# A transformer block whose merge of the memory branch is stored by accumulation, with VectorE's order written out at two stage borders

## The chip, the cores and the metric

The kernel runs on one core of a Trainium2 chip. The metric is the device time of one execution in microseconds (us), the median of several runs. One execution was also recorded by the hardware profiler; its page and its trace are what is quoted here. Engines are named as the page names them: PE is TensorE (matmuls; PEld is its weight load), DVE is VectorE, ACT is ScalarE, POOL is GpSimd, SP is SyncE, which only issues DMAs.

## The reference

One layer of a hybrid block, 512 positions of width 2048, all in float32 (cut to what matters here):

```python
h = rms_norm(x, norm_g)
proj = h @ w_in                       # 13 parts, among them the gates g_conv, g_mla, g_mem
...
o_conv = (b_gate * causal_conv(c_gate * u) * silu(conv_z)) @ w_conv_out
o_mla  = (mla_attention(...) * silu(mla_z)) @ w_mla_out
o_mem  = (memory_attention(...) * silu(mem_z)) @ w_mem_out
merged = sigmoid(g_conv) * o_conv + sigmoid(g_mla) * o_mla + sigmoid(g_mem) * o_mem
x = x + merged @ w_o
```

## The kernel before

**Products.** Every float32 operand is split into two parts that TensorE takes: whi (rounded, by ScalarE) and wlo (the rest, by VectorE, which subtracts whi). A product is three matmuls (L161 whi·xhi, L162 whi·xlo, L163 wlo·xhi). The large products (input projections from w_h, mla_out, w_o) go by panels with seven instead of eight products per 2×2 block: VectorE first forms sums of the raw weight blocks (L263 to L265), then ScalarE rounds (L268) and VectorE subtracts (L269). The left operand goes through the same (pair_sums L243 to L246, pair_split L249 and L250). A panel has four chunks of 42 matmuls, and its results are taken out of four banks (L304 to L314) once all chunks are done. The smaller products (memory K/V, conv_out, mem_out) have plain weights (L154, L155).

**Weights in flight.** SP loads raw weights into three buffers; whi and wlo have two each. `queue` holds the jobs in order, each a generator of two steps (load and sums, then split). `take()` is called at the start of a chunk: it lets the jobs of the next chunks begin, splits the next one, and hands out the weights of the present one. So when chunk k runs, chunk k+1 is split and the sums of k+2 are formed.

**Stages in time.** Memory K/V to about 107 us; input panels (58 of them) to 1320, whose gates go to DRAM (gdram); attention in head groups to 1620 (mla), where the words of ORDER_Q and its like say in which order streams are advanced: `w` a weight product of the next group's projection, `A` and `B` the finishing of old heads, `a` and `b` scores and preparation of new ones; conv_out and memory attention to 1740; mla_out panels to 1908; mem_out in five groups (512, 512, 512, 256 and 256 columns) to 1998; w_o panels to the end. What the three branches add up to lies in DRAM (mgdram): conv_out's results times their gates are stored there (L1040, L1041), mla_out's are added by an accumulating store (L1217, L1218).

**Merge of mem_out.** For each pair of row blocks, `mem_pair` (L1231) loads the gate and the sum so far into one tile "mg" (one buffer), multiplies the banks of mem_out by the gate (L1236), adds the sum so far (L1237), and makes the pair for w_o out of it (sums, then split into xo, L250). It runs step by step beside the next group's matmuls and beside w_o's first panels; xo0 to xo7 are w_o's left operands.

**Who sets the order.** SP and TensorE run in the order in which the program is written (written order, `manual_schedule`); for VectorE a scheduler of the framework sets the order, but for one region of six steps at the first border of the input panels, where the order is the program's. Each engine then works its list in order: an instruction that waits holds up everything behind it. `middle()` of a panel issues the loads of what its results are combined with (gates, the residual xr).

Of the kernel before, what the change touches and what calls it, by code (L numbers as in the profile page):

```python
# [30 lines left out]
P = 128  # L31
# [76 lines left out]
def body(ctx, tc, a, out):  # L108
# [165 lines left out]
    def panel_steps(xp, e, tag, middle=None, tail=None):  # L274
# [235 lines left out]
    def staged_parts():  # L510
# [4 lines left out]
                         (None, None, staged_parts), lambda c: memory_load(c + 1)))  # L515
    work = panels(xp, a["w_h"], len(SEQUENCE), lambda n: make(n), lambda n, e: finish(n, e), "aux")
    queue.insert(32 + 15, [lambda: rotary_weights(), None])
    parts_of_x = all_parts()
    for grp in range(4):
        banks = [bank("acc") for _ in range(2)]  # L520

        for n in dense_units(banks, 512, mT, "T", nk=KB, before=memory_chunk if grp == 0 else None,
                             ahead=lambda c: 2 if 0 < 8 * grp + c - 7 < 23 else 1):
# [39 lines left out]
    for _ in parts_of_x:  # L563
        pass
    close_st()
# [76 lines left out]
    def rotary():  # L642
# [76 lines left out]
        def turned(tag):  # L719
# [4 lines left out]
            nc.gpsimd.dma_start(krdram, kr)  # L724
        later.append(turned)
        yield
# [67 lines left out]
    with tc.manual_schedule(engines={DVE}):  # L794
        for step in range(6):
            next(work)
            if step == 0:
                for i in (6, 7):
                    xp.append(pair_tile(pxb, f"xp{i}"))
                    x_load(i, etile())  # L800
                late_parts = [x_pair(6), x_pair(7)]
            elif step < 5:
                for _ in range(1 + step % 2):
                    next(late_parts[(step - 1) // 2])
# [210 lines left out]

    def gate_blocks(grp):
# [12 lines left out]
        return out  # L1029
# [8 lines left out]
    def conv_result(grp, banks):  # L1038
        for i, sg in enumerate(gate_blocks(grp)):
# [23 lines left out]
    def conv_steps():  # L1063
        for grp in range(4):
            for r in conv_out(grp):
                if r is not None:
                    results[grp] = r
                    if pg is not None:
# [312 lines left out]
```

## Time and profile before

| what | us |
| --- | --- |
| three runs, median (lowest to highest) | 2189.48 (2189.06 to 2191.71) |
| the profiled execution, its time | 2187.3 |
| the profiled execution, its span on the chip | 2185.5 |
| mean granted clock of TensorE in it | 0.992 |

The page begins with each engine's busy time and instruction count. A row of the timeline has start, length, engine, line, operation and out<-in, and in brackets the idle time of the engine just before it and what ended that. A row of the waits has who waited, for whom, the total, the number of times and the longest. A row of the DMA issues has out<-in, queue, count, size and the median time from issue to landing. Here is how the three longest stages with stalls look in the slices of the page, where a digit is the busy share of one fortieth of the span in tenths:

```profile
PE   9989999999999999999999999999999999998799
PEclk9999999999999999999999999999999999999899
```

The dips are in the third slice and in the two slices near the end (mem_out to w_o).

### The profile page before, as it was taken

To read this page: it belongs to the slowest core of one execution; us is meant where nothing else is said; L and a number is where in the kernel's file an instruction comes from. 1 tells how busy PE (TensorE), PEld (TensorE's weight loads), DVE (VectorE), ACT (ScalarE), POOL (GpSimd) and SP (SyncE) were. 2 spreads that over 40 slices of the span, in tenths; PEclk is the share of its full clock that TensorE was granted. 3 is DMA by queue.
4 is the path that set the end of the run, shared out by engine and by line. 5 is a ranking of instruction groups with operands and counts; after the bars stand their busy time and mean duration, and the time that the engine had idled before them with its cause. 6 is when DMAs were issued, how large, how long until landed. Compare 5 with 4: busy or idle time off the path is not lost.

```text
span 2185.5 us, 38852 instructions
## 1 busy us (share of the span) xinstructions
PE 2128.3 (97%) x16040; PEld 2038.7 (93%) x16040; DVE 1741.5 (80%) x2764; ACT 1003.8 (46%) x1219; POOL 123.9 (6%) x173
## 2 busy tenths in 40 slices
PE   9989999999999999999999999999999999998799
PEld 8789999999999999999999999888888799987799
DVE  6986888888888888888888786888877688757787
ACT  6743444344334334444444444877764433323333
POOL 0000000000000000000000001221211100000000
PEclk9999999999999999999999999999999999999899
DMA  8633433333334334343444446222266765554343
GB/s 331 231 106 136 155 136 126 126 126 129 123 126 137 115 129 137 118 141 127 136 136 139 133 136 244 74 82 108 98 231 249 306 186 173 170 204 149 126 147 136
DMA packets 92289, 334.31 MB, mean 153 GB/s; under 512 B 10768, under 2 KB 11024, under 8 KB 90064
## 3 DMA queue, kind: packets, MB, share of 16 engines
q1 hardware_dynamic: 72000, 256.77, 34.4%
q0 software_dynamic: 11616, 51.12, 6.6%
q10 hardware_dynamic: 8496, 23.94, 3.1%
q8 instruction: 125, 2.05, 0.4%
q14 instruction: 52, 0.43, 0.1%
HBM read 273.34 MB, written 58.46 MB: 152 GB/s over the span
## 4 chain that ended last, share of the span: by engine, by line
PE 81%; DVE 8%; DMA 4%; issue 4%; ACT 2%; POOL 0%; SPq 0%; DVEq 0%; POOLq 0%; ACTq 0%
PE acc L161 14%; PE acc L162 14%; PE acc L163 14%; PE aux L163 11%; PE aux L162 11%; PE aux L161 11%; DVE wlo L269 3%; DMA raw<-in_w_mla_out 1%; DMA raw<-in_w_o 1%; DVE raw L263 1%; PE aux L978 1%; DMA sb<-gdram 1%; DMA raw<-in_w_h 1%; PE aux L961 1%; DVE wlo L155 0%
## 5 line engine op out<-in xcount | busy, mean ns | idle before, releaser
L268 ACT ACTIVATE whi<-raw 128x1792 fp32r<-128x1792 f32 x304 | 517.7, 1703 | 793.0 <-PE acc L162 352.8
L269 DVE TENSOR_TENSOR wlo<-raw,whi 128x1792 fp32r<-128x1792 f32 x304 | 614.3, 2021 | 194.2 <-ACT whi L268 193.7
L163 PE MATMUL aux<-xp,wlo 128*128 128x256 f32 (+1 forms) x1712 | 479.5, 280 | 5.0 <-DVE wlo L269 5.0
L161 PE MATMUL aux<-xp,whi 128*128 128x256 f32 (+1 forms) x1712 | 479.8, 280 | 1.0 <-ACT whi L268 1.0
L162 PE MATMUL aux<-xp,whi 128*128 128x256 f32 (+1 forms) x1712 | 480.0, 280 | 0.0
L163 PE MATMUL acc<-xp,wlo 128*128 128x256 f32 x1680 | 469.4, 279 | 3.4 <-DVE wlo L269 3.4
L162 PE MATMUL acc<-xp,whi 128*128 128x256 f32 x1680 | 469.8, 280 | 0.0
L161 PE MATMUL acc<-xp,whi 128*128 128x256 f32 x1680 | 469.3, 279 | 0.0
L163 PEld LDWEIGHTS aux<-xp,wlo 128*128 128x128 f32 (+1 forms) x1712 | 320.4, 187 | 5.6 <-DVE wlo L269 5.6
L161 PEld LDWEIGHTS aux<-xp,whi 128*128 128x128 f32 (+1 forms) x1712 | 321.4, 188 | 1.4 <-ACT whi L268 1.4
L162 PEld LDWEIGHTS aux<-xp,whi 128*128 128x128 f32 (+1 forms) x1712 | 320.9, 187 | 0.0
L163 PEld LDWEIGHTS acc<-xp,wlo 128*128 128x128 f32 x1680 | 314.6, 187 | 4.3 <-DVE wlo L269 4.2
L161 PEld LDWEIGHTS acc<-xp,whi 128*128 128x128 f32 x1680 | 315.6, 188 | 0.0
L162 PEld LDWEIGHTS acc<-xp,whi 128*128 128x128 f32 x1680 | 315.1, 188 | 0.0
L263 DVE TENSOR_TENSOR raw<-raw 128x512 f32<-128x512 f32 x304 | 208.0, 684 | 57.3 <-DMA raw<-in_w_h 29.8
L155 DVE TENSOR_TENSOR wlo<-raw,whi 128x1024 fp32r<-128x1024 f32 (+2 forms) x91 | 101.5, 1119 | 47.7 <-ACT whi L154 47.7
L154 ACT ACTIVATE whi<-raw 128x1024 fp32r<-128x1024 f32 (+2 forms) x91 | 88.9, 977 | 102.6 <-PE acc L162 41.5
L265 DVE TENSOR_TENSOR raw<-raw 128x256 f32<-128x256 f32 x304 | 127.7, 421 | 6.2
L264 DVE TENSOR_TENSOR raw<-raw 128x256 f32<-128x256 f32 x304 | 127.6, 420 | 5.7
L343 POOL TENSOR_TENSOR rs_r<-rs_t,mhalf 128x2 f32<-128x2 f32 (+2 forms) x71 | 69.5, 989 | 270.0 <-DVE rs_t L342 209.6
L161 PE MATMUL acc<-whi,blk 128*128 128x384 f32 (+1 forms) x224 | 84.8, 379 | 0.0
L163 PE MATMUL acc<-whi,blk 128*128 128x384 f32 (+1 forms) x224 | 80.9, 361 | 0.0
(359 smaller groups left out, 3900.9 us busy)
## 6 DMA issues: line engine op xcount, KB each, us to landing
raw<-in_w_h SPq DMA_DIRECT2D x240, 512.0 KB, 3.5
raw<-in_w_mla_out SPq DMA_DIRECT2D x32, 512.0 KB, 3.9
raw<-in_w_o SPq DMA_DIRECT2D x32, 512.0 KB, 3.7
raw<-in_w_mem_kv SPq DMA_DIRECT2D x31, 512.0 KB, 7.2
gdram<-e ACTq DMA_DIRECT2D x22, 512.0 KB, 2.8
raw<-in_w_ukv SPq DMA_DIRECT2D x16, 512.0 KB, 5.6
raw<-in_w_conv_out SPq DMA_DIRECT2D x16, 512.0 KB, 9.0
aadram<-z POOLq DMA_DIRECT2D x8, 896.0 KB, 4.1
```

Source lines behind the costliest of these rows:

```text
L154: act.activation(hi[:, cols], raw[:, cols], AF.Copy)
L155: vec.tensor_tensor(out=lo[:, cols], in0=raw[:, cols], in1=r32(hi[:, cols]), op=ALU.subtract)
L161: nc.tensor.matmul(o, lhsT=s[0], rhs=m[0], start=start, stop=False, skip_group_check=shared)
L162: nc.tensor.matmul(o, lhsT=s[0], rhs=m[1], start=False, stop=False, skip_group_check=shared)
L163: nc.tensor.matmul(o, lhsT=s[1], rhs=m[0], start=False, stop=stop, skip_group_check=shared)
L263: vec.tensor_tensor(out=f[:, 4:6], in0=f[:, 1:3], in1=f[:, 0:1].to_broadcast([P, 2, 256]), op=ALU.add)
L264: vec.tensor_tensor(out=f[:, 6], in0=f[:, 5], in1=f[:, 1], op=ALU.add)
L265: vec.tensor_tensor(out=f[:, 7], in0=f[:, 6], in1=f[:, 3], op=ALU.add)
L268: act.activation(hi, f[:, 1:8], AF.Copy)
L269: vec.tensor_tensor(out=lo, in0=f[:, 1:8], in1=r32(hi), op=ALU.subtract)
L343: pool.tensor_tensor(out=r, in0=t, in1=mhalf[:, :n], op=ALU.pow)
L961: nc.tensor.matmul(sb[:, :n], lhsT=qr[:, cols], rhs=krh[:, :n], start=False, stop=False)
```

## The change

It has eight parts.

1. `take()` gets a list `fills`: pieces of VectorE's work that are put between the split of chunk k+1 and the sums of chunk k+2, one per chunk. The beginning of a job is a function of its own, `begin`.
2. From step 27 of memory K/V to the sixth step of the input panels, VectorE's order is the program's (`manual_dve`). The last two pairs of x (xp6, xp7) are four fills there. Weight buffers of their own ("staged") are used at entries 0, 3, 6 and so on instead of 2, 5, 8, the look-ahead of two starts at step 8 and ends after step 30, and the first panel's jobs begin before the stage's end (`begin(2)`).
3. ORDER_Q, ORDER_Q1 and ORDER_LAST: a weight product stands between `B` and the first score `a`, and in the first group two more products stand ahead of the scores; the later runs of `w` are shorter by as much.
4. A panel's `middle()` is called at its second chunk before the weights are taken, not at the third chunk after.
5. The rotary transposes of the latents are made available one step later (`yield` ahead of `later.append`).
6. The gate loads of conv_out are written apart from the multiplications (`gate_blocks(grp)` fills `gates_of`).
7. The tile "my" of the memory attention has four buffers instead of two.
8. mem_out: each group is multiplied by its gates as soon as it is done (L1277), out of the banks into the gate tile, which is added to mgdram by an accumulating store (L1278). The gates are loaded ahead (L1260) into three slots that take the place of xo7; the sum is read back (L1271) into the places of xo6 and xo5 (pairs 0 to 4), into "merge" (5 and 6) or a tile of its own (7). The pairs are made three steps later. L1237 is gone. VectorE's order is the program's from the beginning of mem_out to the ninth chunk of w_o (n == 8). A w_o panel's addition of the residual becomes a fill.

The diff, without some of the smaller moves:

```diff
-ORDER_Q = "a a a B a a a 4w a w b b 5w a 4w a w a a w"
+ORDER_Q = "a a a B w a a a 3w a w b b 5w a 4w a w a a w"
 ORDER_KV1 = "16w"
-ORDER_Q1 = "4w a a 2w a 2w a a a w a w b b 4w a w a w a a"
-ORDER_LAST = "a a a B a a a 4w a w b b", "5w a 4w a w a a w"
+ORDER_Q1 = "6w a a w a 2w a a a w a w b b 3w a w a w a a"
+ORDER_LAST = "a a a B w a a a 3w a w b b", "5w a 4w a w a a w"
...
+    fills = []
+
     def upcoming(*jobs):
         queue.extend([job, None] for job in jobs)
 
+    def begin(at):
+
+        if at < len(queue) and queue[at][1] is None:
+            queue[at][1] = queue[at][0]()
+            queue[at].append(next(queue[at][1]))
+
     def take(ahead=1):
-        for at, entry in enumerate(queue[:2 + ahead]):
-            if entry[1] is None:
-                entry[1] = entry[0]()
-                entry.append(next(entry[1]))
-            if at <= ahead and entry[2] is None:
+        for at, entry in enumerate(queue[:1 + ahead]):
+            begin(at)
+            if entry[2] is None:
                 entry[2] = next(entry[1])
+        if fills:
+            fills.pop(0)()
+        begin(1 + ahead)
         return queue.pop(0)[2]
 
...
+            if c == 1 and middle is not None:
+                middle()
             whi, wlo = take()
             if c == 2:
                 while later:
                     later.pop(0)("aux" if tag == "acc" else "acc")
-                if middle is not None:
-                    middle()
...
-                         (None, None, staged_parts), lambda c: memory_load(c + 1)))
+                         (staged_parts, None, None), lambda c: memory_load(c + 1)))
...
+    manual_dve = ExitStack()
     for grp in range(4):
         banks = [bank("acc") for _ in range(2)]
...
             c, step = n // 4, 8 * grp + n // 4
+            if step == 27:
+                manual_dve.enter_context(tc.manual_schedule(engines={DVE}))
...
+    begin(2)
...
             nc.gpsimd.dma_start(krdram, kr)
+        yield
         later.append(turned)
-        yield
```

```diff
-                    next(late_parts[(step - 1) // 2])
+    for i in (6, 7):
+        xp.append(pair_tile(pxb, f"xp{i}"))
+        x_load(i, etile())
+        steps = x_pair(i)
+        fills += [lambda steps=steps: (next(steps), next(steps)), lambda steps=steps: next(steps)]
+    for _ in range(6):
+        next(work)
+    manual_dve.close()
...
 
     def conv_result(grp, banks):
-        for i, sg in enumerate(gate_blocks(grp)):
+        for i, sg in enumerate(gates_of[grp]):
...
     for head in range(2):
         mem_q[head] = memory_queries(head)
+    gate_blocks(0)
     conv_result(0, results[0])
     run(ORDER_TAIL, w=conv, a=new[0], b=new[1])
...
-            t = pq.tile([P, 2, S], F32R, tag="my", name="my", bufs=2)
+            t = pq.tile([P, 2, S], F32R, tag="my", name="my", bufs=4)
...
+    manual_dve.enter_context(tc.manual_schedule(engines={DVE}))
...
+    def place(n, name):
+        return px.tile([P, 2, 7, H], F32R, tag=f"xo{n}", name=name, bufs=1)
+
+
+
+    gplace = r32(place(7, "gt")).rearrange("p a s n -> p (a s n)")
+    gates = [gplace[:, 1024 * i:1024 * (i + 1)].rearrange("p (f n) -> p f n", f=2) for i in range(3)]
+    mplace = {0: 6, 1: 5, 2: 6, 3: 5, 4: 6}
+
+    def gate_load(n):
+        if n < NP:
+            nc.gpsimd.dma_start(gates[n % 3], gdram[16 + n])
+
...
+    def gated(n, banks):
+        gt = gates[n % 3]
         for i in range(2):
-            vec.tensor_tensor(out=two(t, 4)[:, i], in0=banks[i], in1=two(t, 4)[:, i], op=ALU.mult)
-        vec.tensor_tensor(out=two(t), in0=two(t), in1=two(t, 4), op=ALU.add)
-        yield
-        yield from pair_parts(t, xp[n])
-
-    def mem_pairs(n, banks):
-        for i in range(len(banks) // 2):
-            yield from mem_pair(n + i, banks[2 * i:2 * i + 2])
+            vec.tensor_tensor(out=gt[:, i], in0=banks[i], in1=gt[:, i], op=ALU.mult)
+        nc.gpsimd.dma_start(mgdram[n], gt, accum_op=ALU.add)
+
+    def pair_out(n, t):
+        pair_sums(t)
+        yield
+        x = place(n, f"xo{n}")
+        xp.append(x)
+        pair_split(t[:, 1:8], x)
+        yield
+
+    def pairs_out(*ns):
+        ts = []
+        for n in ns:
+            ts.append(merged(n))
+        for n in ns:
+            gate_load(n + 3)
+        for _ in range(3):
+            yield
+        for n, t in zip(ns, ts):
...
-        done += width // 256
+        ns = [done + i for i in range(width // 256)]
+        for i, n in enumerate(ns):
+            gated(n, banks[2 * i:2 * i + 2])
+        done += len(ns)
+        if done <= 6:
+            for _ in pairs:
+                pass
+            pairs = pairs_out(*ns)
+    for _ in pairs:
+        pass
     close_am2()
```

```diff
     def finish_o(n, e):
+        fills.append(lambda: result(n, e))
+
...
-        next(pairs, None)
+    last = [merged(n) for n in (6, 7)]
+    fills += [lambda: None, lambda: None]
+    for n, t in zip((6, 7), last):
+        steps = pair_out(n, t)
+        fills += [lambda steps=steps: next(steps)] * 2
+    for n, _ in enumerate(work):
+        if n == 8:
+            manual_dve.close()
     close_e()
     close_m()
```

The lines of the program after the change differ by some 9 to 17 from those before: L269 is L278 after, L263 to L265 are L272 to L274, L243 to L246 are L252 to L255, L250 is L259, L961 is L971.

**VectorE at the mem_out border, before.** From the last weights of mem_out to the wait before 2036 us in the trace of before: w_o's sums of raw weights (L263 to L265) and splits (L269), and between them the merge of pair 5 or 6 (L1236, L1237, L243 to L246, and the split L250).

```order
L263 TENSOR_TENSOR raw<-raw 128x512
L264 TENSOR_TENSOR raw<-raw 128x256
L1236 TENSOR_TENSOR mg<-aux,mg 128x512 x2
L265 TENSOR_TENSOR raw<-raw 128x256
L1237 TENSOR_TENSOR mg<-mg 128x1024
L269 TENSOR_TENSOR wlo<-raw,whi 128x1792
L263 TENSOR_TENSOR raw<-raw 128x512
L243 TENSOR_TENSOR mg<-mg 128x512
L264 TENSOR_TENSOR raw<-raw 128x256
L244 SCALAR_TENSOR_TENSOR mg<-mg 128x256
L265 TENSOR_TENSOR raw<-raw 128x256
L246 TENSOR_TENSOR mg<-mg 128x256
```

Every merge is multiplied, added and split in one row, and the next pair's multiplication comes behind it.

**VectorE at the same place, after.** From the end of group 4 (the two L1277 take its pair out of the banks) to the split of pair 5, just ahead of the first split of w_o's weights.

```order
L1277 TENSOR_TENSOR gt<-aux,gt 128x512 x2
L155 TENSOR_TENSOR wlo<-raw,whi 128x512
L259 TENSOR_TENSOR xo_21793<-mg,xo_21793 128x1792
L155 TENSOR_TENSOR wlo<-raw,whi 128x512
L252 TENSOR_TENSOR mg<-mg 128x512
L253 SCALAR_TENSOR_TENSOR mg<-mg 128x256
L255 TENSOR_TENSOR mg<-mg 128x256
L155 TENSOR_TENSOR wlo<-raw,whi 128x512
L272 TENSOR_TENSOR raw<-raw 128x512
L273 TENSOR_TENSOR raw<-raw 128x256
L274 TENSOR_TENSOR raw<-raw 128x256
L259 TENSOR_TENSOR xo_21836<-mg,xo_21836 128x1792
```

The multiplication by the gate no longer stands among w_o's sums and splits pair by pair; the sums of mg (L252 to L255), which need the read-back, stand in fixed places between the weight splits, and behind w_o's sums (L272 to L274) comes the split of a pair and then that of the weights. Three chunks further on, VectorE's rows after the change read:

```order
L278 TENSOR_TENSOR wlo<-raw,whi 128x1792
L272 TENSOR_TENSOR raw<-raw 128x512
L273 TENSOR_TENSOR raw<-raw 128x256
L274 TENSOR_TENSOR raw<-raw 128x256
L278 TENSOR_TENSOR wlo<-raw,whi 128x1792
```

There sums and split of the same weights follow each other directly; before, parts of a pair mostly stood between them.

**GpSimd through mem_out, before.** Its queue issues these loads, two for each pair.

```order
L1218 DMA mgdram<-sg 128x1024 x8
L1233 DMA mg<-gdram 128x1024
L1234 DMA mg<-mgdram 128x1024
L1233 DMA mg<-gdram 128x1024
L1234 DMA mg<-mgdram 128x1024
```

Each load of a pair waits for the one tile mg.

**GpSimd through mem_out, after.** "gt" is a gate slot; L1235 is mla_out's accumulating store.

```order
L1235 DMA mgdram<-sg 128x1024 x7
L1260 DMA gt<-gdram 128x1024 x3
L1235 DMA mgdram<-sg 128x1024
L1278 DMA mgdram<-gt 128x1024 x2
L1271 DMA mg<-mgdram 128x1024
L1260 DMA gt<-gdram 128x1024
L1271 DMA mg<-mgdram 128x1024
L1260 DMA gt<-gdram 128x1024
```

Three gate loads moved ahead of mla_out's last store, and behind each group come its two accumulating stores, then the read-backs with a gate load between.

**VectorE at the first border, before.** In the input panels' first chunks; e is the tile of pair 6 of x, whose scaling (L484) and sums (L243 to L246) are one step of it.

```order
L269 TENSOR_TENSOR wlo<-raw,whi 128x1792
L263 TENSOR_TENSOR raw<-raw 128x512
L264 TENSOR_TENSOR raw<-raw 128x256
L265 TENSOR_TENSOR raw<-raw 128x256
L484 TENSOR_TENSOR e<-e,xscale 128x1024
L243 TENSOR_TENSOR e<-e 128x512
L244 SCALAR_TENSOR_TENSOR e<-e 128x256
L246 TENSOR_TENSOR e<-e 128x256
L269 TENSOR_TENSOR wlo<-raw,whi 128x1792
```

Between the sums of a chunk's raw weights and their split L269 stands the part of x.

**The same place, after.** The same instructions, for pair 7 of x.

```order
L278 TENSOR_TENSOR wlo<-raw,whi 128x1792
L493 TENSOR_TENSOR e<-e,xscale 128x1024
L252 TENSOR_TENSOR e<-e 128x512
L253 SCALAR_TENSOR_TENSOR e<-e 128x256
L255 TENSOR_TENSOR e<-e 128x256
L272 TENSOR_TENSOR raw<-raw 128x512
L273 TENSOR_TENSOR raw<-raw 128x256
L274 TENSOR_TENSOR raw<-raw 128x256
L278 TENSOR_TENSOR wlo<-raw,whi 128x1792
```

The part of x has moved ahead of the sums of the next raw weights, and sums and split follow each other.

More of the change, by code (lines that the diff above doesn't have):

```diff
@@ L522, in body @@
         for n in dense_units(banks, 512, mT, "T", nk=KB, before=memory_chunk if grp == 0 else None,
-                             ahead=lambda c: 2 if 0 < 8 * grp + c - 7 < 23 else 1):
+                             ahead=lambda c: 2 if 8 <= 8 * grp + c < 31 else 1):
             if n % 4 < 3:
@@ L1014, in body @@
     pg, close_g = None, None
+    gates_of = {}
     def gate_blocks(grp):
@@ L1028, in gate_blocks @@
             out += [t[:, 0], t[:, 1]]
-        return out
+        gates_of[grp] = out
     def conv_out(grp):
@@ L1249, in body @@
         late_blocks.append(t)
+    for n in range(3):
+        gate_load(n)
     pairs = iter([])
@@ L1262, in body @@
                 next(pairs, None)
-        for _ in pairs:
-            pass
-        pairs = mem_pairs(done, banks)
-        done += width // 256
+        ns = [done + i for i in range(width // 256)]
[8 more added lines that the diff above has]
+        pass
     close_am2()
@@ L1298, in tail_o @@
         nc.sync.dma_start(out[15 * P:16 * P], xr[:, 1])
-    for _ in work:
-        next(pairs, None)
+    last = [merged(n) for n in (6, 7)]
[6 more added lines that the diff above has]
+            manual_dve.close()
     close_e()
```

32 lines of the change are left out of this document (17 added, 15 removed).

## The prediction

> **What bounds the kernel now.** I read the page's busy table first, then a window of an undisturbed stage and windows of the last stages, then the waits of TensorE, then the single rows of TensorE where those waits are.
>
> ```profile
> span 2185.5 us, 38852 instructions
> PE 2128.3 (97%) x16040; PEld 2038.7 (93%) x16040; DVE 1741.5 (80%) x2764; ACT 1003.8 (46%) x1219; POOL 123.9 (6%) x173
> 600.00:660.00 60.00, 60.00 (x511) 60.00 (x511) 51.62 (x72) 23.82 (x18) 0.53 (x1) 1.00 0.37 123
> 1710.00:1740.00 30.00, 27.21 (x113) 22.03 (x113) 19.87 (x19) 14.53 (x11) 3.26 (x6) 0.94 0.92 376
> 1740.00:1770.00 30.00, 26.50 (x205) 25.68 (x204) 23.76 (x29) 8.91 (x6) 2.18 (x4) 0.94 0.51 172
> 1908.00:1998.00 90.00, 87.91 (x384) 71.49 (x384) 54.46 (x66) 26.40 (x25) 7.18 (x13) 1.00 0.47 162
> 1998.00:2073.00 75.00, 54.34 (x423) 53.61 (x422) 57.01 (x76) 22.78 (x15) 2.09 (x4) 0.86 0.42 150
> PE aux L161 <- DVE mg L1236: 15.0, 2, 14.4
> PE acc L161 <- DVE mg L1236: 5.7, 1, 5.7
> PE aux L961 <- DVE qr L948: 2.3, 7, 0.3
> ```
>
> A window's columns are start:end and length, busy time and count of PE, PEld, DVE, ACT and POOL, the granted clock, the DMA share and GB/s. TensorE is busy for 97% of the span and has no gap at all in the undisturbed minute 600 to 660, where 511 matmuls take 60 us: 0.117 us each. A panel chunk is 42 of them, 4.94 us; a mem_out chunk is 24 or 12 matmuls of 512 columns, by the 384 of window 1908 to 1998 5.46 or 2.73 us. So the change can only pay where TensorE stands still or runs at a reduced clock, and all of it together is 2185.5 − 2128.3 = 57 us of idle time, plus some 10 us for the reduced clock. The largest single place is the border between the memory projection (mem_out) and the output projection (w_o): 2.1 us idle in mem_out's own 90 us, 20.7 us in the 75 us behind it at a mean clock of 0.86, and two waits for the multiplication at L1236, 5.7 and 14.4 us.
>
> ```profile
> 2005.01 0.58 PE L161 MATMUL acc<-xo,whi 128*128 128x256 f32 x1 [5.66 <-DVE mg L1236]
> 2036.87 0.58 PE L161 MATMUL aux<-xo,whi 128*128 128x256 f32 x1 [14.40 <-DVE mg L1236]
> 2032.30 0.53 POOL L1233 DMA_DIRECT2D mg<-gdram  x1 [14.79 <-DVE xo L250]
> 2036.12 1.29 DVE L1236 TENSOR_TENSOR mg<-aux,mg 128x512 f32<-128x512 f32 x2 [4.12 <-DMA mg<-gdram]
> ```
>
> Here a w_o panel wants banks that still hold a mem_out group. They come free with L1236, whose gate is loaded into the only mg buffer (2032.30), and that load waits for the split L250 of the pair before. Gate load, multiplication, sums and split run one after another, pair by pair, while TensorE waits.
>
> **The mem_out border.** The change multiplies each group out of its banks at once (L1277) with a gate loaded earlier, and sends the product by an accumulating store (L1278) into DRAM. The read-back L1271 comes later, into places of its own. So the two waits above, with their restarts, go: 5.66 and 14.40, and about 4 us of the half clock behind them. What is late next? VectorE's order, now fixed: the sums of mg stand in it ahead of the weight splits of later chunks, and so TensorE waits for the read-back through VectorE. I walked the new order with these rows:
>
> ```profile
> L269 DVE TENSOR_TENSOR wlo<-raw,whi 128x1792 fp32r<-128x1792 f32 x12 | 24.3, 2021 | 8.0 <-ACT whi L268 8.0
> L155 DVE TENSOR_TENSOR wlo<-raw,whi 128x1024 fp32r<-128x1024 f32 (+1 forms) x19 | 18.8, 994 | 11.8 <-ACT whi L154 11.8
> L263 DVE TENSOR_TENSOR raw<-raw 128x512 f32<-128x512 f32 x13 | 8.9, 685 | 6.0 <-DMA raw<-in_w_o 6.0
> L264 DVE TENSOR_TENSOR raw<-raw 128x256 f32<-128x256 f32 x13 | 5.4, 418 | 0.2
> L1237 DVE TENSOR_TENSOR mg<-mg 128x1024 f32<-128x1024 f32 x8 | 9.8, 1220 | 0.9 <-DMA mg<-mgdram 0.8
> L268 ACT ACTIVATE whi<-raw 128x1792 fp32r<-128x1792 f32 x304 | 517.7, 1703 | 793.0 <-PE acc L162 352.8
> mgdram<-sg POOLq DMA_DIRECT2D x8, 512.0 KB, 8.5
> mg<-mgdram POOLq DMA_DIRECT2D x8, 512.0 KB, 4.7
> mg<-gdram POOLq DMA_DIRECT2D x8, 512.0 KB, 3.7
> ```
>
> The accumulating store exists already (mgdram<-sg): 8.5 us from issue to landing, against 4.7 and 3.7 for plain reads of the same size. At the 376 GB/s of window 1710 to 1740, 512 KB is 1.4 us, so 2.3 of the 3.7 are issue and completion. That leaves 8.5 − 2.3 = 6.2 us of transfer for an accumulating store as the upper bound, and 4.7 − 2.3 = 2.4 as the lower. The 8.5 was seen beside mla_out's weight loads and this stage has fewer, so I take 4.0, the middle.
>
> A group of 512 columns then reads back at its end + 1.3 (two multiplications) + 1.5 (issue) + 2×4.0 (both stores of the group, which share the engines) + 2.6 (the read) = 13.4 us, and its second pair 3.4 us later, a gate load between them. Four chunks of such a group are 21.8 us and those of a 256 group 10.9, so early groups have room and late ones have not. Let 0 be the start of mem_out. Group 2 ends at 43.7; its pair would land at 57 but sits behind the splits of group 1's second pair and lands at 59.5. Its sums (0.685 + 2×0.42 = 1.5) and one weight split (1.14) end at 62.2, where TensorE wanted it at 60.3: 1.6 us lost at group 3's last chunk. By the same steps, xo3's split and four multiplications (2.4) stand ahead of a weight split of group 4: 3.0 lost. Pair 4 lands at 83.7, its sums, two multiplications and a weight split end at 87.1, wanted at 83.9: 2.8 lost. w_o's first chunk has the sums of pair 5, its own sums and the split of xo5 ahead: 2.3.
>
> In w_o the order itself costs. Per chunk VectorE does the sums (1.5), then the split (1.95 from start to start), and between them it has nothing else to do while ScalarE rounds: 1.70 and 0.17 to reach it. That is 5.4 us against TensorE's 4.94. Each chunk with a part of a pair between (1.5 for sums or 1.95 for a split) takes about 7.2. Three bare chunks lose 0.45 each (1.4), four with pairs 6 and 7 lose 2.2 to 2.4 (9.2), two with an evacuation 3.0 in all. The new total is 0.2 + 1.6 + 3.0 + 2.8 + 2.3 + 1.4 + 9.2 + 3.0 = 23.5 us.
>
> Before, the same stretch (the two windows 1908 to 2073, 384 matmuls of mem_out and the 420 of ten w_o chunks) takes 164.9 us for 136.8 of TensorE's work (12×5.46 + 8×2.73 + 10×4.94): 28.1 lost. **So the border gains 4.6 us**, not the 25 that the two waits suggest; L1237's 9.8 us on VectorE go too and are in the walk. With 2.4 us per store the walk gives −13, with 6.2 +8. New stalls of 1.6 to 3.0 us can halve the clock, which the stretch in w_o hides behind VectorE but the three in mem_out don't; rows for that:
>
> ```profile
> 1716.86 0.50 PE L163 MATMUL aux<-blk,wlo 128*128 128x512 f32 x1 [2.79 <-DVE wlo L155]
> 1717.89 0.63 PE L161 MATMUL aux<-blk,whi 128*128 128x512 f32 x1
> 145.77 0.39 PE L163 MATMUL aux<-xp,wlo 128*128 128x256 f32 x1 [2.17 <-DVE wlo L269]
> 146.11 0.28 PE L162 MATMUL aux<-xp,whi 128*128 128x256 f32 x1
> ```
>
> After the gap of 2.79 a matmul takes 0.63 in place of 0.39; after 2.17 none slows. A stretch of half clock is 3.4 us, 1.5 lost. I count one: +1.5 (0 to +4.5). [...]
>
> **The attention groups.** One weight product is moved between the preparation B and the first score.
>
> ```profile
> 1405.86 0.39 PE L961 MATMUL aux<-krh,qr 128*128 128x256 f32 x1 [0.33 <-DVE qr L948]
> 1406.08 0.29 PE L962 MATMUL aux<-krl,qr 128*128 128x256 f32 x1
> 1406.20 0.28 PE L958 MATMUL aux<-kTh,qTh 128*128 128x256 f32 x1
> PE aux L350 <- ACT kn L863: 1.4, 2, 1.0
> ```
>
> The wait of 0.33 costs 0.59 from start to start: 0.33, 0.16 by which a matmul's 0.28 exceeds its spacing of 0.12, and 0.10 for the slow start (0.22 against 0.12). Seven times: −4.1. The moved product is three matmuls of 384 or 512 columns, over 0.5 us, so the cover is there; what was left behind is one product fewer later, whose row shows no wait (0 to +2). In the first group two products are moved to the front, over waits of 1.4 us for ScalarE (L350), of which the larger is 1.0: −1.0 (0 to −1.7).
>
> **Conv_out, memory attention, gates.** TensorE loses 2.8 us in 1710 to 1740 and 3.5 in 1740 to 1770, and at granted clock 0.94 (0.06 of 60 us) some 3.6 more. The 2.79 above is a weight split L155 that stood behind two of L1040's multiplications; now both splits stand ahead of the four multiplications. Around 1741 and 1754:
>
> ```profile
> 1741.58 0.39 PE L163 MATMUL acc<-xm,wlo 128*128 128x256 f32 x1 [1.26 <-DVE wlo L269]
> 1754.51 0.38 PE L163 MATMUL acc<-xm,wlo 128*128 128x256 f32 x1 [1.63 <-DVE wlo L269]
> ```
>
> the first weights of mla_out are prepared up to one split earlier. I take the 2.79 with its restart and half clock (−4.5) and 1.8 of the 1.26 + 1.63: **−6.3** (−2 to −10, nearly all that is lost there). The gate loads themselves do not come sooner: GpSimd's queue has them at the same places as before, only their place in the program's text changed. ScalarE's wait for the two "my" buffers goes too, but TensorE isn't behind it: 0.
>
> **mla_out's loads.** SP's loads of gates and of xr stand two weight loads earlier, so a panel's weights no longer wait behind them.
>
> ```profile
> DVE raw L263 <- DMA raw<-in_w_mla_out: 12.6, 5, 3.6
> 1800.00:1830.00 30.00, 29.45 (x250) 29.25 (x250) 24.42 (x35) 10.99 (x8) 0.84 (x1) 1.00 0.57 172
> 1830.00:1860.00 30.00, 28.66 (x245) 28.21 (x244) 24.65 (x32) 10.61 (x7) 1.70 (x2) 1.00 0.62 186
> ```
>
> TensorE is idle for 0.55 + 1.34 = 1.9 us, two restarts make 2.4: −2.4, if the same delay isn't just met by the weight load two places earlier (then 0).
>
> **The first border** (memory K/V to the input panels) has VectorE's order written out too.
>
> ```profile
> 107.84 0.38 PE L161 MATMUL aux<-xp,whi 128*128 128x256 f32 x1 [1.01 <-ACT whi L268]
> 110.25 0.58 PE L163 MATMUL aux<-xp,wlo 128*128 128x256 f32 x1 [1.91 <-DVE wlo L269]
> 152.46 0.38 PE L163 MATMUL acc<-xp,wlo 128*128 128x256 f32 x1 [1.48 <-DVE wlo L269]
> 124.62 2.02 DVE L269 TENSOR_TENSOR wlo<-raw,whi 128x1792 fp32r<-128x1792 f32 x1
> ```
>
> The first weights are ready earlier, which takes the 1.01, the 1.91 and 1.5 of half clock; but the parts of x (pair 6 and 7) now come before the sums of the next weights, where before they stood between these sums and their split and hid ScalarE's 1.87 us (124.62 shows no wait). Five chunks meet this, and VectorE has 7.2 to 8.1 us to do in 4.94. Walked in the same way, the last of the first two panels' chunks ends 2.4 us later than before: **+2.4** (−5 to +5). The rotary part that goes a yield later moves one split past rows on which nothing waits: 0.
>
> **Sum.** +2.4 − 4.1 − 1.0 − 6.3 − 2.4 − 4.6 + 1.5 = −14.5 us. The profiled execution took 2187.3 (span 2185.5 and 1.8 around it), so 2172.8; the runs' median is 2189.48, 2.2 above it, so 2175.0.
>
> **Rivals.**
> (a) The border works as a whole: stores are as fast as reads (2.4 us per 512 KB: −13), or VectorE's order never falls behind since its stock of weights covers it. Then the mem_out border brings −13 to −25, with the rest −10 more: 2154 to 2166. For it: VectorE is busy only 57 of 75 us there now. Against: in the old order too L269 waits 8.0 us for L268 in this stretch. Chance 0.25.
> (b) The read-back takes the place of the bank wait: the accumulating store needs 6.2 us or more of transfer. Then each group's pair lands some 4 to 5 us later, the sums of mg hold up VectorE in every group, the border is +8 rather than −4.6, the first border at +5, and gates and loads bring only −3: 2189.5 + 8 + 5 − 5 − 3 = 2194. It decides at about 4.8 us per store, where the border is at 0, and at 6.2 the whole is slower. The row of 8.5 speaks for it. [...] Chance 0.10.
> (c) The change does not do what it says at the gates, as GpSimd's order is the same, and mla_out's delay only moves: then −14.5 + 6.3 + 2.4 − 2 = −8, 2182, or, with the first border at its worst, about 2187, no change. Chance 0.20, of which a good half is no measurable change.
>
> **How the numbers follow.** My forecast of 2175 (2168 to 2182 by itself) has 0.45. A measurement here can tell 0.2%, 4.4 us: below 2185.1 is faster. Faster: 0.45 + 0.25 + 0.08 = 0.78; same: 0.12; slower: 0.10. The range goes from the middle of (a), 2154, down to 2153, and up to 2191, short of (b).
>
> **What would show it.** Right: no row of TensorE waits for L1277 over 1 us; rows of L163 or L161 wait for L155 and L278 in 1960 to 2070, 1.5 to 3 us each, with VectorE there waiting for mg<-mgdram and for whi; mgdram<-gt lands in about 6 to 7 us. The waits L961 <- qr are gone, the 2.79 at 1717 too; between 120 and 160 TensorE idles more than before, with L278 waiting for whi. Wrong: no waits of L278 for whi in w_o, or a store that lands in under 5 or over 8.5 us; gates loaded earlier than before; a border that loses under 12 or over 30 us.

## The result, and the profile after

The changed kernel takes 2225.39 us (median of 4 runs, 2222.01 to 2229.68) against 2190.6 us (2189.06 to 2194.58) of the kernel before: a ratio of 1.0157, with a 95% interval of 1.0133 to 1.0181. It is **35 us slower**, where 15 us faster was forecast and the range ended at 2191.

The same head of the page, and the waits that are new or longer (TensorE's in the attention groups, and those of SP's DMA queue in the stage of mla_out):

```profile
span 2221.8 us, 38855 instructions
PE 2144.4 (97%) x16040; PEld 2056.2 (93%) x16040; DVE 1740.4 (78%) x2756; ACT 1006.7 (45%) x1219; POOL 131.1 (6%) x181
PE acc L161 <- ACT kn L873: 14.3, 5, 3.0
PE acc L161 <- DVE vl L134: 2.8, 1, 2.8
SPq L1228 <- DMA mgdram<-sb: 16.7, 2, 16.0
SPq L1228 <- DMA mgdram<-sg: 12.4, 1, 12.4
```

VectorE and ScalarE do as much as before; TensorE has the same 16040 matmuls. Its waits for L1236 are gone, as they should be, and so are the seven of 0.33 for qr. In their place stand six waits of 2.8 to 3.0 us for ScalarE and VectorE, and SP, which only issues loads, waits 16.0 and 12.4 us at two of its gate loads (L1228). These last rows are the first to look at where weights come late: the weight loads written behind such a gate load were issued after it (1821.54 and 1823.37 below).

Where the time came from is read by cutting the trace at TensorE's first or last matmul of a stage. us in each stage, of the profiled executions (by this cut the input panels and attention of the kernel before end at 1335.4 and 1634.5, some 15 us later than the times given with the kernel):

| kernel | to the end of the input panels | attention | conv_out, memory | mla_out | mem_out | w_o |
| --- | --- | --- | --- | --- | --- | --- |
| before, first profile | 1335.4 | 299.1 | 105.4 | 167.9 | 90.3 | 182.6 |
| before, second profile | 1341.6 | 299.1 | 102.7 | 166.3 | 90.4 | 190.2 |
| after | 1342.1 | 320.3 | 103.7 | 177.3 | 94.0 | 179.5 |

The second profile of before is a run of the experiments below. Two stages have the loss, beyond all scatter: attention +21.2 and mla_out +9.4 to +11.0. mem_out and w_o together take 273.5, against 273.0 and 280.6.

The attention groups in TensorE's rows, at one of the six places:

```profile
1452.65 0.44 PE L161 MATMUL acc<-whi,blk 128*128 128x384 f32 x1 [2.83 <-DVE vl L134]
1451.40 1.65 DVE L134 SCALAR_TENSOR_TENSOR vl<-acc,kr__97,vh 128x256 fp32r<-128x256 f32 x4
1451.97 2.17 ACT L873 ACTIVATE kn<-acc,rs_r 128x128 f32<-128x128 f32 x8 [0.56 <-DVE vl L134]
```

The moved weight product writes into a bank "acc". The four banks of that name hold the group's new keys and values until vl and kn have been read out of them, and the first comes free just ahead of 1452.65. Behind the product, in TensorE's order, stand the scores, which need other banks and could have run.

And mla_out, where one of SP's gate loads stands in the way:

```profile
1832.20 0.39 PE L161 MATMUL acc<-xm,whi 128*128 128x256 f32 x1 [2.48 <-ACT whi L277]
1836.79 0.58 PE L163 MATMUL acc<-xm,wlo 128*128 128x256 f32 x1 [4.07 <-DVE wlo L278]
1821.54 0.33 SPq L1228 DMA_DIRECT2D sg<-gdram  x1
1823.37 13.72 SPq L271 DMA_DIRECT2D raw<-in_w_mla_out  x4
1828.67 0.69 DVE L272 TENSOR_TENSOR raw<-raw 128x512 f32<-128x512 f32 x1 [3.98 <-DMA raw<-in_w_mla_out]
```

The stalls are in the third panel's weights (the expectations below call them the fifth's). The third panel's gate load is issued at 1821.54, when the store that frees its buffer (one of two) has landed; the weight loads behind it start at 1823.37, VectorE stands for 3.98 us, and TensorE for 2.48 and 4.07.

### The profile page after: what moved, and what is told of

It is laid out like the page before. It is cut to its first block, busy times and chain, and to the rows that moved or that the text cites. A ratio compares the mean times of both kernels' runs of the same rounds, so it can differ in the third digit from the quotient of the medians.

```text
span 2221.8 us, 38855 instructions
## 1 busy us (share of the span) xinstructions
PE 2144.4 (97%) x16040; PEld 2056.2 (93%) x16040; DVE 1740.4 (78%) x2756; ACT 1006.7 (45%) x1219; POOL 131.1 (6%) x181
## 5 line engine op out<-in xcount | busy, mean ns | idle before, releaser
L278 DVE TENSOR_TENSOR wlo<-raw,whi 128x1792 fp32r<-128x1792 f32 x304 | 614.6, 2022 | 213.9 <-ACT whi L277 213.6
L272 DVE TENSOR_TENSOR raw<-raw 128x512 f32<-128x512 f32 x304 | 208.2, 685 | 55.8 <-DMA raw<-in_w_h 33.3
L155 DVE TENSOR_TENSOR wlo<-raw,whi 128x1024 fp32r<-128x1024 f32 (+2 forms) x89 | 100.5, 1130 | 61.0 <-ACT whi L154 60.9
L274 DVE TENSOR_TENSOR raw<-raw 128x256 f32<-128x256 f32 x304 | 128.1, 422 | 6.7
L161 PE MATMUL acc<-whi,blk 128*128 128x384 f32 (+1 forms) x224 | 86.1, 385 | 17.1 <-ACT kn L873 14.3
```

Of the source, the lines that this page charges most:

```text
L155: vec.tensor_tensor(out=lo[:, cols], in0=raw[:, cols], in1=r32(hi[:, cols]), op=ALU.subtract)
L161: nc.tensor.matmul(o, lhsT=s[0], rhs=m[0], start=start, stop=False, skip_group_check=shared)
L272: vec.tensor_tensor(out=f[:, 4:6], in0=f[:, 1:3], in1=f[:, 0:1].to_broadcast([P, 2, 256]), op=ALU.add)
L274: vec.tensor_tensor(out=f[:, 7], in0=f[:, 6], in1=f[:, 3], op=ALU.add)
L278: vec.tensor_tensor(out=lo, in0=f[:, 1:8], in1=r32(hi), op=ALU.subtract)
```

## The experiments

**1. The order strings alone, undone and alone done.** In the changed kernel the three strings were set back; in the kernel before only they were set new.

```diff
-ORDER_Q = "a a a B w a a a 3w a w b b 5w a 4w a w a a w"
+ORDER_Q = "a a a B a a a 4w a w b b 5w a 4w a w a a w"
...
```

> The changed kernel with the three order strings of before (ORDER_Q, ORDER_Q1, ORDER_LAST), nothing else. Theory (the weight product moved ahead of the scores needs a bank that still holds the group's keys and values, so it waits 2.8 us for ScalarE's kn and VectorE's vl, in six groups, and these gaps halve the clock): the waits of acc L161 for kn and vl go, the seven waits of 0.3 us for qr come back, and the time falls by 18 to 23 us, to about 2204. Rival (ScalarE's evacuation is the bound of the groups, whichever instruction waits for it): TensorE waits as long elsewhere in each group, and the time stays within 5 us of the changed kernel's 2225.

> The kernel before with only the three new order strings. Theory (as for e1): 2190 + 18 to 23 us, about 2210, with waits of 2.8 us of acc L161 for kn or vl in six groups. Rival (the wait comes from an interplay with the other parts of the change, for instance the rotary step or a late start): the time stays within 5 us of 2190.

Undone: 2202.0 us, 23.4 less; the attention stage takes 299.1 again, to the tenth as before. Done alone: 2210.08 against 2192.09 (ratio 1.0082, interval 1.0063 to 1.0101), 18 more, and the stage takes 320.4. The waits of TensorE, first undone, then done alone:

```profile
PE aux L971 <- DVE qr L958: 2.3, 7, 0.3
...
PE acc L161 <- ACT kn L863: 17.1, 6, 3.0
```

The one edit takes away seven waits of 0.3 and makes six of 2.8. Nothing else of the change is needed for it. The waits are the same in every kernel with the new strings, 17.1 us in all; the stage was longer where its granted clock was lower. In the kernels with the new strings that took 317.6 (experiment 4), 320.3 (the change) and 323.2 us (experiment 3) for the stage, its mean granted clock was 0.97, 0.96 and 0.95.

**2. A weight product one place later.** If the bank comes free at a fixed time, the wait must shrink by what is put in front of it. In the first kernel of experiment 5 the product was put behind the second score.

```diff
-ORDER_Q = "a a a B a a a 4w a w b b 5w a 4w a w a a w"
+ORDER_Q = "a a a B a a w a 3w a w b b 5w a 4w a w a a w"
...
```

> As c1_three_undone (2174.3), but in ORDER_Q and ORDER_LAST one weight product stands behind the second score and not behind the third. Theory (the product's bank comes free about 2.8 us after the place ahead of the first score, and two scores take 1.2 us): the product waits about 1.3 us (with the 0.33 for qr back in front of it) in each of six groups, with or without a half clock: 7 to 14 us slower than c1, about 2184. Rival (the bank wait arises only where the product comes directly behind B): within 3 us of c1.

2180.99 us, 6.7 over its base, just under what was expected. The two ratios to the kernel before, 0.9952 (0.9936 to 0.9968) and 0.993 (0.9916 to 0.9944), overlap at their ends, so the stage decides: attention takes 304.4, where the kernels with the old strings have 299.1 to 299.2. So 5.3 us are here. TensorE's rows and waits:

```profile
PE acc L161 <- ACT kn L873: 4.4, 6, 0.7
PE aux L971 <- DVE qr L958: 2.3, 7, 0.3
1446.11 0.44 PE L161 MATMUL acc<-whi,blk 128*128 128x384 f32 x1 [0.74 <-ACT kn L873]
```

The wait is 2.8 us ahead of the scores, 0.74 behind two (1.3 was expected) and absent behind three: a bank that comes free at its own time, not something that only the place behind B has.

**3. The loads of mla_out.** middle() back at its old place; and, apart from that, middle() early as in the change, but the gate load issued by GpSimd.

```diff
-            if c == 1 and middle is not None:
-                middle()
             whi, wlo = take()
             if c == 2:
...
+                if middle is not None:
+                    middle()
```

> The changed kernel with middle() back at a panel's third chunk, behind take(). Theory (SP's gate load sg waits for the store of its buffer, 16.0 us at the first panel and 12.4 us at the third, and the weight loads stand behind it in SP's queue): SP's waits at that load fall below 5 us each, TensorE's stalls of 2.5 and 4.1 us in the fifth panel's weights go, and the time falls by 6 to 11 us, to about 2217. Rival (the weights are late there because the DMA queues are full of stores, not because of SP's order): the stalls stay and the time falls by less than 3 us.

```diff
-            nc.sync.dma_start(sgs[n], gdram[8 + n])
+            nc.gpsimd.dma_start(sgs[n], gdram[8 + n])
```

> The changed kernel, with middle() early as in the change, but the gate load sg issued by GpSimd instead of SP. Theory (it is SP's queue: weight loads stand behind a gate load that waits for its buffer): the weight loads are issued in time though the gate load waits as before; TensorE's two stalls of 2.5 and 4.1 us in mla_out go, and the time falls by 6 to 11 us, to about 2217, as with middle() at its old place. Rival (the early gate loads delay the weights through the DMA engines' bandwidth): the stalls stay, under 3 us.

2215.41 and 2212.92 us: 10.0 and 12.5 less, the second a little more than was expected. mla_out takes 164.0 and 162.1, below both profiles of before. SP's waits at the gate load with middle() at its old place, and then TensorE's longest waits from 1760 to 1850 us in the changed kernel, with middle() at its old place, and with the gate load on GpSimd:

```profile
SPq L1228 <- DMA mgdram<-sb: 4.8, 2, 4.2
SPq L1228 <- DMA mgdram<-sg: 2.9, 1, 2.9
...
PE acc L163 <- DVE wlo L278: 6.4, 3, 4.1
...
PE acc L163 <- DVE wlo L278: 2.6, 3, 1.6
...
PE acc L163 <- DVE wlo L278: 2.4, 2, 1.6
```

From 16.7 and 12.4 to 4.8 and 2.9, and TensorE has neither of the two stalls. In the second kernel the third panel's gate load is issued at 1821.55, as in the change (1821.54); only the weight loads no longer stand behind it. So it is the queue, not the engines' bandwidth.

**4. Where the fill stands.** Two statements of take() exchanged, so that a part of x or of a pair lies between the sums of a chunk and its split.

```diff
+        begin(1 + ahead)
         if fills:
             fills.pop(0)()
-        begin(1 + ahead)
```

> The changed kernel with the fill put behind the sums of chunk k+2 instead of ahead of them (two statements of take() exchanged). Theory (in the order split, fill, sums, split VectorE waits 1.9 us for ScalarE's rounding at every chunk of the two borders): the rows in which L163 waits 1.55 us for wlo go for chunks with a fill, at the first border and in w_o, and the time falls by 10 to 16 us, to about 2212. Rival (VectorE has simply too much to do at the borders, 7 us in a chunk of 4.94, whatever its order): under 4 us change.

2210.88 us, 14.5 less. VectorE in w_o, in the changed kernel and then with the fill last:

```profile
2060.84 2.02 DVE L278 TENSOR_TENSOR wlo<-raw,whi 128x1792 fp32r<-128x1792 f32 x1 [1.91 <-ACT whi L277]
2068.22 2.03 DVE L278 TENSOR_TENSOR wlo<-raw,whi 128x1792 fp32r<-128x1792 f32 x1 [1.90 <-ACT whi L277]
2070.30 0.39 PE L163 MATMUL aux<-xo,wlo 128*128 128x256 f32 x1 [1.56 <-DVE wlo L278]
...
2055.57 2.02 DVE L259 TENSOR_TENSOR xo<-mg,xo 128x1792 fp32r<-128x1792 f32 x1
2057.56 2.03 DVE L278 TENSOR_TENSOR wlo<-raw,whi 128x1792 fp32r<-128x1792 f32 x1
2063.01 2.03 DVE L278 TENSOR_TENSOR wlo<-raw,whi 128x1792 fp32r<-128x1792 f32 x1 [0.39 <-ACT whi L277]
```

VectorE does the same work in both; the 1.9 us for ScalarE's rounding lies open in the first and is covered by the fill in the second. Of the 12.4 us by which the two profiles differ, 4.9 stand at the end of the input panels and 5.1 are in w_o, the two places with fills; mem_out loses 1.2. Another 2.7 are in attention, which has the same six waits and a higher granted clock (0.97 against 0.96): these are not the edit's.

**5. All three at once, then the first border too, then mem_out alone.**

> The changed kernel with all three edits of the first runs at once: the order strings of before, middle() at its old place, the fill behind the sums. If the three causes are separate, their gains add up: 2225.4 - 23.4 - 10.0 - 14.5 = 2177.5, some 13 us under the kernel before (2190.6). If they share a cover (for instance because a stall that goes lets the next engine become late), less is left of it, down to the same as before.

> As c1_three_undone, and the first border as before (staged weights at entries 2, 5 and so on, the written order of VectorE for six steps only, parts of x behind the chunks). Theory (at the first border the loss was nearly all the order split, fill, sums, which c1 has undone already): within 3 us of c1. Rival (the staged weights and the longer written order cost something of their own): 3 to 7 us faster than c1.

> The kernel before with part 8 alone (mem_out gated out of the banks, accumulating stores, read-back into free places, written order there), and the fill behind the sums. Theory (the bank waits go, read-back stalls of 2.5 us stay in mem_out and single late splits in w_o): 5 to 8 us under the kernel before, about 2184. Rival (the gain of this part is larger and was eaten elsewhere): 15 us or more under it. Rival (the read-back takes it all): within 2 us of it.

> The kernel before, unchanged, with a second profile. In its first profile w_o's last 18 chunks took 4.76 us each, in those of all other kernels 4.95. If that is a property of the execution and not of the kernel, this profile shows 4.95 there, a span 3 to 5 us above 2185.5, and stage differences against the first profile overstate the loss by as much.

| kernel | us, median | ratio to before (95%) |
| --- | --- | --- |
| the three edits undone or exchanged | 2174.33 | 0.993 (0.9916 to 0.9944) |
| and the first border as before | 2179.98 | 0.9944 (0.9929 to 0.9958) |
| and all else but mem_out as before | 2178.34 | 0.9945 (0.9924 to 0.9965) |

The sum of the three gains was 47.9, so 2177.5 was expected; 51.1 came: within the scatter the three gains add up, so the causes are separate. The kernel before is beaten by 17 us. The second and third rows don't differ by more than their intervals; that the border as before is the slower by 5.7 (the intervals just overlap) was expected by neither theory. It speaks against the rival: the change's first border, with the fill last, costs nothing of its own and may be worth a little. mem_out alone, with the fill last, brings 13.3 us (of 2191.63). That is more than the 5 to 8 that were expected and less than the 15 of the rival, but its interval, 7.7 to 16.7, does not part the two.

The kernel before, profiled again, has a span of 2195.1, 9.6 more than the first; single profiles of one kernel differ by that much here, though attention takes 299.1 in both. 3 to 5 more were expected: the chunks of 4.95 in w_o did come, but 6.2 us more stand already at the end of the input panels.

**6. The accumulating store by itself.** A plain store in its place, which leaves out the sum of the other two branches.

```diff
-        nc.gpsimd.dma_start(mgdram[n], gt, accum_op=ALU.add)
+        nc.gpsimd.dma_start(mgdram[n], gt)
```

> As c1_three_undone, with a plain store of mem_out's gated result instead of an accumulating one; this leaves out the sum of the other two branches. Theory of the prediction (the accumulating store is slow, 6.3 us from issue to landing, a plain one about 3.7, and the read-back waits for it): store lands in under 4.5 us, and TensorE's two stalls of 2.5 and 2.1 us in mem_out fall below 1 us. Rival (issue on GpSimd, completion and the read itself make most of the way): the store lands in 4.5 to 5.5 us and the stalls stay over 1.3 us.

One run: 2169.72 us. The DMA issues, with the accumulating store (the first kernel of 5) and with the plain one, and ahead of them the first kernel's waits of TensorE for L155 in mem_out, of which the second has none:

```profile
PE aux L163 <- DVE wlo L155: 4.5, 2, 2.5
PE acc L163 <- DVE wlo L155: 1.0, 1, 1.0
mgdram<-gt POOLq DMA_DIRECT2D x8, 512.0 KB, 5.6
...
mgdram<-gt POOLq DMA_DIRECT2D x8, 512.0 KB, 3.1
```

mem_out takes 87.1 in place of 96.8, and its stalls, 5.5 us in all, are gone; its granted clock is 1.00 in place of 0.96, which is most of the rest. So the theory of the prediction holds, as far as one run shows: the read-back of an accumulated result is what is left of mem_out's cost.

**7. Early gate loads on a free queue.** In the first kernel of experiment 5, middle() early and the gate load on GpSimd.

> As c1_three_undone (old order strings, fill behind the sums), but middle() early as in the change, with the gate load sg issued by GpSimd. Theory (earlier loads are worth something once no weight load stands behind a waiting one): 1 to 4 us under c1, about 2172. Rival (part 4 has no value of its own, since SP was never the bound with the loads at their old place): within 1.5 us of c1's 2174.3.

2175.6 us, with a ratio of 0.9922 (0.9899 to 0.9945): the same as 2174.3, the rival's case. The earlier load gives nothing measurable once it does no harm.

## Why the prediction was wrong

**The attention groups (−4.1 and −1.0 forecast; +21.2 measured).** This is the step that failed most. The prediction looked at what the moved product hides ("over 0.5 us, so the cover is there") and at what it leaves behind ("whose row shows no wait"), and never asked what the product itself waits for at its new place. It needs a bank, and three scores further on the bank was free just in time, without a wait in any row of before. What it needs was in the trace of before, VectorE's vl and ScalarE's kn and the product behind them:

```profile
1441.54 1.65 DVE L134 SCALAR_TENSOR_TENSOR vl<-acc,kr__97,vh 128x256 fp32r<-128x256 f32 x4
1442.11 2.17 ACT L863 ACTIVATE kn<-acc,rs_r 128x128 f32<-128x128 f32 x8 [0.56 <-DVE vl L134]
1442.79 0.44 PE L161 MATMUL acc<-whi,blk 128*128 128x384 f32 x1
```

The seven waits of 0.33 did go, as forecast; six of 2.83 to 2.96 took their place, and clock was lost behind five of the six (0.66 or 0.83 over ten us there, against 1.00 behind the sixth). In the first group the wait of 0.98 went too, as forecast; two of 0.19 and 0.20 took its place.

**mla_out's loads (−2.4 forecast, "then 0" as the other end; the whole stage +9.4 to +11.0 measured).** The prediction reckoned only what no longer stands in front of the weight loads at the old place. It didn't ask what the gate load waits for at the new one: its buffer, which a store has to release. The weight loads behind it in SP's queue were issued only after its wait, 12.4 us at the third panel. The rows of the queue's own waits, which the prediction does not show, have this load waiting 4.5 and 2.9 us in all already before:

```profile
SPq L1211 <- DMA mgdram<-sb: 4.5, 2, 3.9
SPq L1211 <- DMA mgdram<-sg: 2.9, 1, 2.9
```

**The gates (−6.3 forecast).** conv_out and memory took 103.7, against 105.4 and 102.7: nothing. The stall of 2.79 at 1716.86 on which −4.5 rested is 1.58 in the second profile of before, and in its place after stands another of 1.96 for the split of p. mla_out gives nothing clear either: in the profiles of the five kernels that have this part of the change and the loads at the old place it takes 164.0 to 167.0, and in the four that have neither this part nor the new loads (before twice, experiment 1's second, mem_out alone) 165.9 to 167.9. So no part of the 6.3 is shown. The wording that the change "does not do what it says at the gates" was the better case.

**The mem_out border (−4.6, and +1.5 for the clock).** This step held in the main. In the changed kernel mem_out begins and w_o's eleventh chunk begins at

```profile
1943.48 0.40 PE L161 MATMUL acc<-am,whi 128*128 128x512 f32 x1
2104.90 0.38 PE L161 MATMUL acc<-xo,whi 128*128 128x256 f32 x1 [2.21 <-ACT whi L277]
```

so mem_out and ten chunks took 2104.90 − 2.21 − 1943.48 = 159.2 us; the walk gave 160.3, and 161.8 with the clock. (Two of the walk's terms don't follow from its own times: 62.2 − 60.3 is 1.9 and not 1.6, and 87.1 − 83.9 is 3.2 and not 2.8. With them it gives 161.0. And 87.91 us for 384 matmuls make a chunk of 5.49 rather than 5.46, which counts alike before and after.) The waits on the two banks went, and the late splits came: gaps of 0.85, 2.51 and 2.45 in mem_out (1.6, 3.0, 2.8 forecast); w_o's second to fourth chunks took 5.5 us each (5.4 forecast) and the next four 6.9 to 7.4 (7.2 forecast). The store took 5.5 us to land, 6.3 were taken. The half clock that was counted for mem_out did not come: from 1943 to 2037 the granted clock was 1.00. (The 3.4 us and the 1.5 of that term are those of one place in the trace of before: behind the 2.79, from 1717.89 to 1721.30, eight matmuls stand 0.43 apart in place of 0.23, and the granted clock from 1718 to 1721 is 0.50.) But the walk ends too soon. Behind it TensorE waits the 2.21 us, and the eleventh chunk takes 8.33; in the first profile of before the eleventh and the thirteenth lose 1.0 and 1.5. By the end of the thirteenth chunk the gain over that profile is about 2.8 us, near the 3.1 that were forecast with the clock, but partly because the clock's term that didn't come and the late loss cancel. So most of the 25 us that the two waits suggest was handed back to VectorE, by the order, and exchanging two statements (experiment 4) gets a part of it.

**The first border (+2.4).** It held too, as far as it can be told: to the end of the input panels 1342.1 us, and 1341.0, 1343.1 and 1342.7 in the three experiments with the same border; 1335.4 to 1341.9 in the five profiles with the old one (mean 1339.2, so about +3); 1334.3 to 1339.0 with the fill last.

**The rivals.** A slower kernel had a chance of 0.10, for the read-back's price (b). The read-back wasn't it. Of (a), only the border's −13 is near to a measurement, the −13.3 of mem_out alone in experiment 5, and that with the fill last; even with the three edits taken back the kernel takes 2174.3, not 2154 to 2166. Of (c), the gates' half came; mla_out's delay did more than move.

In all, attention misses its forecast by 26.3 us, mla_out by some 12.6 and the gates by 6.3: 45 of the 50 us between 2175.0 and 2225.39.

## What to carry to other kernels

When an instruction is moved ahead in an engine's order, ask first what it will wait for there (a bank, a buffer, a store that frees it), and then who stands behind it in that queue; a row without a wait at the old place says nothing of the new one, where here six waits of 2.83 to 2.96 us arose. Read the waits of the queue that only issues loads: here a gate load waited 12.4 us for its buffer, and the weight loads behind it were late. And in an order written by hand, put other work between a step that feeds another engine and the step that takes its answer; here it covered 1.9 us of waiting for ScalarE.

## What was not expected of the hardware

The same matmuls went at two rates, 0.113 and 0.117 us each, at a granted clock of 1.00. In w_o's last chunks the kernel before has in its first profile, and then in its second (window, then busy time and count of PE and the rest, with the clock ahead of the last two columns):

```profile
2095.00:2176.00 81.00, 81.00 (x716) 81.00 (x715) 69.26 (x93) 30.55 (x21) 0.00 (x0) 1.00 0.47 153
2095.00:2180.00 85.00, 85.00 (x724) 85.00 (x724) 71.67 (x98) 30.50 (x21) 0.00 (x0) 1.00 0.49 159
...
1893.00:1931.00 38.00, 38.00 (x338) 38.00 (x337) 30.14 (x39) 13.78 (x10) 3.88 (x6) 1.00 0.69 209
1880.00:1920.00 40.00, 40.00 (x342) 40.00 (x341) 33.66 (x45) 14.83 (x11) 1.70 (x2) 1.00 0.65 189
```

That is 0.113 and 0.117 us for one matmul, 4% apart, with no gap and the clock at 1.00 in both; a chunk takes 4.76 or 4.95. These are two executions of one program, and part of the difference of 9.6 us between the two profiles is from it (18 chunks at 0.19 are 3.4). Nor is it only in w_o: the last two rows are from mla_out, of the kernel of experiment 3 with the gate load on GpSimd (0.112) and of the changed kernel (0.117). Those 338 matmuls would take 39.5 us at 0.117, so most of the 1.9 us between 162.1 and 164.0 in experiment 3 is from it. What set it stays open.

Around five of the six waits of 2.83 to 2.96 us in the changed kernel the granted clock fell to 0.50 for some us. These are windows of ten us around the six, in order of time, with the granted clock ahead of the last two columns, and then four shorter ones in them.

```profile
1410.00:1420.00 10.00, 7.04 (x38) 6.79 (x37) 8.01 (x22) 6.93 (x23) 1.28 (x2) 0.83 0.03 11
1450.00:1460.00 10.00, 7.35 (x46) 7.10 (x47) 7.31 (x23) 7.46 (x24) 0.59 (x1) 1.00 0.23 92
1488.00:1498.00 10.00, 8.18 (x33) 7.97 (x34) 6.07 (x18) 6.10 (x18) 0.59 (x1) 0.66 0.24 92
1526.00:1536.00 10.00, 7.17 (x37) 6.88 (x36) 7.66 (x21) 7.44 (x23) 0.90 (x2) 0.83 0.22 88
1567.00:1577.00 10.00, 8.64 (x36) 8.38 (x37) 5.76 (x19) 5.31 (x18) 0.59 (x1) 0.66 0.24 94
1606.00:1616.00 10.00, 7.80 (x38) 7.54 (x39) 6.88 (x21) 6.24 (x19) 0.59 (x1) 0.83 0.23 92
...
1414.00:1417.00 3.00, 2.98 (x12) 2.98 (x13) 2.44 (x7) 1.73 (x7) 0.00 (x0) 0.50 0.00 0
1417.50:1420.00 2.50, 2.50 (x16) 2.46 (x15) 1.64 (x8) 1.62 (x6) 0.59 (x1) 1.00 0.11 46
1489.50:1495.50 6.00, 5.68 (x21) 5.68 (x22) 4.40 (x14) 3.83 (x14) 0.59 (x1) 0.50 0.23 86
1496.00:1498.00 2.00, 2.00 (x12) 1.79 (x11) 0.17 (x1) 0.85 (x3) 0.00 (x0) 1.00 0.31 125
```

Around the second wait, of 2.83 us, the clock stayed at 1.00. Around the first, fourth and sixth (2.96, 2.83 and 2.83 us) it was 0.83 over the ten, which at 0.50 makes 3.4 us; around the third and fifth (2.83 us each) it was 0.66, which makes 6.8. The same length of wait came with all three; what parted them is not shown.
